# A hybrid encoder layer: token-major attention product, state-group output matrices on VectorE, two-level recurrence

## The chip, the cores and the metric

One core of a Trainium2 chip runs the whole layer as one program. TensorE (PE in the profile) multiplies matrices, its weight loads are listed apart as PEld, VectorE (DVE) and ScalarE (ACT) do elementwise work, GpSimd (POOL) does some more, and SyncE (SP) issues transfers. The metric is the device time of one execution in microseconds (us).

## The reference

One layer with 256 tokens of width 2048 in float32. `w_in` projects to q, k, v and u, each 1024 wide. Three things matter here. The attention group has 16 heads of 64:

```python
scores = einsum(q, k) * 64 ** -0.5 + rel_bias          # band of 64-token chunks, masked
probs = softmax(scores)
out = einsum(probs, v)
```

The state group has 64 channel groups, each driving a 64-dim complex diagonal state, with the pairs (state, group) spread over 128 partitions and 32 columns:

```python
s[l] = a * s[l-1] + B u[l]                             # complex, a per state
y = Re(C s) + d_skip * u ;  y = gelu(y) ; y = y * sigmoid(y @ w_glu + b_glu)
```

Both outputs pass an RMS norm over all 1024 channels, are concatenated, multiplied by `w_out` and added to `alpha * x`; then come a layer norm, a gated FFN of width 5632 with a causal convolution over three tokens, and a second layer norm.

## The kernel before

Weights stream from HBM in chunks of 128 x 1024 float32. Each chunk is split so that two fast products stand for a float32 one: ScalarE casts it to a high part (`hi`, L163), VectorE subtracts to get the low part (`lo`, L164), and TensorE multiplies both (L209 with 512 moving columns and L211 with 256, eight times per chunk, in `mm_a`; L245, L247, L249 in `mm_b`). 104 such chunks make up the first 400 us: v (numbers 0 to 7 and 24 to 31), u (8 to 23), kq (32 to 63: four for each pair of heads, two for k and two for q), then `w_out`'s attention half (64 to 79), the gate of the state group (80 to 87), `w_out`'s state half (88 to 103). The FFN follows, to 1150 us.

`run` (L167) walks over the chunks: it splits chunk j+3, starts the transfer of chunk j+7, issues chunk j's products, and then lets every side job issue one step. Side jobs are generators: parameters of the state group, local states (`s5_loc`, whose products `ll`, L764, are slipped between a chunk's products), stacked kernels, output matrices (`s5_cm`, L909 to L914, on GpSimd), the recurrence (`s5_scan`, L819 to L822) and one attention job for each pair of heads. `paced` deals out a list of small operations, so many us of them per step. Four pairs of hi and lo buffers are in flight. A scheduler then sorts the instructions of each engine by readiness and priority, so that chunks 38 and 39 stand before 36 and 37 on TensorE, and 42 before 40; on the chip each engine works down its own list strictly in order.

The state group cuts the 256 tokens into 64 blocks of 4. `ll` gives each block's own end state; the recurrence then walks over the 64 blocks, 63 steps of four VectorE operations on 128 x 64 elements, each element of `X` 256 bytes from the next. `s5_y` multiplies entering states (`X`) by the output matrices (`CM`) and adds the block's own part.

An attention job for a pair of heads: scores (`S`, L1012, L1013), bias and row maximum on VectorE (L1021, L1022), exponentials on ScalarE (L1024), division by the row sums on VectorE (L1029, L1031), transposes on TensorE (`T`, L1036 to L1038), copy to `pT` (L1040), product with v (`O`, L1048, L1050): weights are v's 64 columns of a head, the moving matrix is `pT` with 256 and then 128 tokens. The result is channel-major, as `w_out`'s product wants it. Its squares are summed on GpSimd (`sqa`, L979), and four TensorE products with a column of ones give the RMS norm (L990). Float32 products on TensorE count as two instructions in the profile.

Of the kernel before, what the change touches and what calls it, by code (L numbers as in the profile page):

```python
# [12 lines left out]
F32 = mybir.dt.float32  # L13
# [3 lines left out]
ALU = mybir.AluOpType  # L17
# [101 lines left out]
class Builder:  # L119
# [172 lines left out]
    def plan_phase1(self):  # L292
# [155 lines left out]
        self.sqa = ap.tile([P, SEQ], F32, name="sqa")  # L448
# [24 lines left out]
    def evac_u(self, f, ps):  # L473
        nc = self.nc
        t = self.evac_ab(ps, f"ub{f}")
        u = self.t1([P, 4, 64], f"ut{f}")
        nc.vector.tensor_tensor(u[:, ::-1].rearrange("p t c -> p c t"), ps[:, 0:SEQ].rearrange("p (c t) -> p c t", t=4),
                                t.rearrange("p (c t) -> p c t", t=4), op=ALU.add)
        with self.tc.high_priority(300):
            self.put_u(f, u)  # L480

# [67 lines left out]
    def s5_params(self):  # L549
# [152 lines left out]
        cA = self.cA = ap.tile([P, 2, NP_], F32, name="cA")  # L702
        cB = self.cB = ap.tile([P, 2, NP_], F32, name="cB")
        ops.append((0.2, lambda: V.tensor_copy(cA[:, 0], PA[:, 0, 3])))
        ops.append((0.2, lambda: V.tensor_copy(cA[:, 1], PA[:, 0, 3])))
        ts(cB[:, 0], PA[:, 1, 3], -1.0, MUL)
        ops.append((0.2, lambda: V.tensor_copy(cB[:, 1], PA[:, 1, 3])))

        ts(self.sc[:, 1], self.sc[:, 1], -1.0, MUL)
        yield from self.paced(ops, 1.7)  # L710
# [27 lines left out]
    def s5_loc(self):  # L738
# [20 lines left out]
        def ll(q, ri):  # L759
            def mm(i, g2):  # L760
                if i == 0 and g2 == 0:
                    st[1] = self.bank((3, 4)[ri], f"ll{q}{ri}")
                r = slice(64 * g2, 64 * g2 + 64)
                nc.tensor.matmul(st[1][r, 64 * i:64 * i + 64], lhsT=loc[:, q % 2, ri, i, r], rhs=self.up[:, q * 8 + i],  # L764
                                 start=True, stop=True, tile_position=(0, 64 * g2))

            def evac():
                nc.scalar.copy(self.X[:, ri, q * 8:q * 8 + 8], st[1].rearrange("p (i c) -> p i c", c=64))
            for i in range(8):
                for g2 in range(2):  # L770
                    put(lambda i=i, g2=g2: mm(i, g2), 0.25)
            put(evac, 0)
# [15 lines left out]
        while self.mb_ready < 4 or self.up_ready < 1:  # L788
            yield
        self.X = bp.tile([P, 2, NP_, 64], F32, tag="d2", name="X")  # L790
        yield from drained()
        yield
        both(ll, 0)
# [13 lines left out]
        yield  # L807

    def s5_scan(self):
        while not self.loc_done:  # L810
            yield
        V, X, ap = self.nc.vector, self.X, self.ap_

        def step(c):
            s = X[:, :, :, c]
            t = X[:, :, :, c + 1]
            u = ap.tile([P, 2, NP_], F32, tag="su", bufs=2, name=f"su{c}")
            w = ap.tile([P, 2, NP_], F32, tag="sw", bufs=2, name=f"sw{c}")
            V.tensor_tensor(u, s[:, ::-1], self.cB, op=ALU.mult)  # L819
            V.tensor_tensor(w, s, self.cA, op=ALU.mult)  # L820
            V.tensor_tensor(u, u, t, op=ALU.add)
            V.tensor_tensor(t, w, u, op=ALU.add)  # L822
# [53 lines left out]

    def s5_cm(self):
        nc, bp, ap = self.nc, self.bp, self.ap_
        Gp = nc.gpsimd
        self.CM = []  # L880
        while not self.par_done:
            yield
# [3 lines left out]
        for pg in range(4):  # L886
# [19 lines left out]
            ci = self.sc[:, 1, pr].unsqueeze(2).broadcast_to(sh)  # L906
            for ri in range(2):

                Gp.tensor_tensor(t0, cr if ri == 0 else ci, ar, op=ALU.mult)  # L909
                Gp.tensor_tensor(t1, ci if ri == 0 else cr, ai, op=ALU.mult)  # L910
                for g2 in range(2):
                    r = slice(64 * g2, 64 * g2 + 64)
                    o = self.CM[pg][r, ri].rearrange("p c (e g q) -> p g c e q", g=2, q=SG)[:, g2]
                    Gp.tensor_tensor(o, t0[r], t1[r], op=ALU.add if ri == 0 else ALU.subtract)  # L914
                yield
            self.cm_ready = pg + 1

    def s5_y(self):
        nc, bp = self.nc, self.bp
        X, Kt, CM, up = self.X, self.Kt, self.CM, self.up  # L920
        for pg in range(4):
            while self.cm_ready <= pg:
                yield
            if pg == 0:
                ysh = self.ysh = bp.tile([P, 8, SEQ], F32, tag="d4b", name="ysh")
            ps = self.bank((3, 4)[pg % 2], f"y{pg}")
            for f in range(2):
                for i in range(4):
                    m = slice(32 * i, 32 * i + 32)
                    for t in range(3):  # L930
                        for r in range(4):
                            l = 4 * f + r
                            pr = 8 * pg + l
                            o = ps[32 * r:32 * r + 32, f * SEQ + i * 64:f * SEQ + (i + 1) * 64]
                            if t == 0:
                                a = dict(lhsT=Kt[:, pr // 16, m, pr % 16], rhs=up[:, pr])
                            else:
                                a = dict(lhsT=CM[pg][:, t - 1, l, m], rhs=X[:, t - 1, pr, 0:63])
                                o = o[:, 1:64]
                            nc.tensor.matmul(o, start=t == 0, stop=t == 2, tile_position=(0, 32 * r), **a)  # L940
                nc.vector.tensor_copy(ysh[:, 2 * pg + f].rearrange("p (c i) -> p i c", i=4),
                                      ps[:, f * SEQ:(f + 1) * SEQ].rearrange("p (i c) -> p i c", i=4))
# [41 lines left out]

    def rms(self, w):
        nc = self.nc
        acc = (self.sqa, self.sqs)[w]
        ps = self.bank((7, 7)[w], f"rms{w}")
        for tt in range(2):
            nc.tensor.matmul(ps[:, tt:tt + 1], lhsT=acc[:, tt * P:(tt + 1) * P], rhs=self.ones, start=True, stop=True)  # L990
        r = self.rs[:, 2 * w:2 * w + 2]
        half = (1.0, 0.5)[w]
        nc.scalar.activation(r, ps[:, 0:2], AF.Sqrt, bias=self.eps, scale=half * half / AW)
        nc.vector.reciprocal(r, r)
        if w == 1:
            nc.vector.tensor_scalar(r, r, half, None, op0=ALU.mult)
        yield


    def attention(self, j):  # L1000
# [12 lines left out]
            nc.tensor.matmul(ps[:, 256:384], lhsT=qt[:, 0:P], rhs=kz[h][:, 0:P], start=True, stop=True)  # L1013

        def soft(h):
            ps, b = st["S", h], st["b", h]
            s = ap.tile([P, 384], F32, tag="sT", bufs=2, name=f"sT{j}{h}")
            m = ap.tile([P, 8], F32, tag="mx", bufs=2, name=f"mx{j}{h}")
            spans = ((0, 256), (256, 384))
            for t, (a, e) in enumerate(spans):  # L1020
                nc.vector.tensor_tensor_reduce(s[:, a:e], ps[:, a:e], b[:, 256 - (e - a):], 1.0, -3e38, ALU.add, ALU.max, m[:, t:t + 1])  # L1021
            nc.vector.tensor_scalar(m[:, 2:4], m[:, 0:2], -1.0, None, op0=ALU.mult)  # L1022
            for t, (a, e) in enumerate(spans):
                nc.scalar.activation(s[:, a:e], s[:, a:e], AF.Exp, bias=m[:, 2 + t:3 + t], accum_out=m[:, 4 + t:5 + t])  # L1024
            st["s", h], st["m", h] = s, m

        def norm(h):
            s, m = st["s", h], st["m", h]
            nc.vector.reciprocal(m[:, 6:8], m[:, 4:6])  # L1029
            for t, (a, e) in enumerate(((0, 256), (256, 384))):  # L1030
                nc.vector.tensor_scalar(s[:, a:e], s[:, a:e], m[:, 6 + t:7 + t], None, op0=ALU.mult)  # L1031

        def trans(h):
            s = st["s", h]
# [32 lines left out]
        yield  # L1067
        soft(0)
        yield
        norm(0)  # L1070
        soft(1)
        yield
        trans(0)
        norm(1)
        yield
        pv(0)
        trans(1)
        if j < 7:
            yield
        pv(1)  # L1080
        yield
        while self.cm_ready < 4:
            yield
# [255 lines left out]
```

## Time and profile before

| | us |
|---|---|
| median of 3 runs | 1151.32 (1151.24 to 1151.71) |
| profiled execution, its own time | 1152.07 |
| its span in the trace | 1150.3 |
| busy in the span: TensorE | 1115.6 (97%) |
| VectorE | 775.0 (67%) |
| ScalarE | 563.4 (49%) |
| GpSimd | 123.3 (11%) |

The shares are means over stages with different limits. The page also gives 40 slices of 28.8 us, each digit a tenth; the lowest busy digit of TensorE behind the first slice, 5, is that of slice 6 (143.8 to 172.5 us).

### The profile page before, as it was taken

Reading aid. Unit: us, or ns where it says so; the run is one execution under the profiler, and the core shown is the slowest. Engines: PE = TensorE matmul, PEld = TensorE weight load, DVE = VectorE, ACT = ScalarE, POOL = GpSimd, SP = SyncE. Lnnn points to the kernel's source line nnn. Section 1 sums busy time; section 2 is a strip of 40 time slices with the busy share of each in tenths; the row PEclk is TensorE's granted clock in tenths of the full one; section 3 lists DMA queues with packets and bytes.
Section 4 is the critical chain, followed back from the end, with each engine's and each line's share of the span. In section 5 each row is a group of like instructions: output and inputs, shape, how many; then the busy total and the mean of one; then the engine's idle time right before and its main releaser. Section 6 shows DMA issues by size and latency. Waiting matters only on the chain.

```text
span 1150.3 us, 17982 instructions
## 1 busy us (share of the span) xinstructions
PE 1115.6 (97%) x6936; PEld 944.2 (82%) x6936; DVE 775.0 (67%) x1379; ACT 563.4 (49%) x849; POOL 123.3 (11%) x113
## 2 busy tenths in 40 slices
PE   8999959999999999999999999999999999999996
PEld 6887748887787888888888888888888888888885
DVE  7993399995678876666666666666666475454555
ACT  5454325553667465555555555555555343343450
POOL 2031870000002000000000000000000550000002
PEclk9999979999999999999999999999999999999998
DMA  8886324553566456666666666666656876666661
GB/s 301 277 236 156 102 87 130 156 155 104 215 192 192 162 163 185 184 185 187 190 187 186 186 185 187 191 185 184 184 185 188 319 211 195 198 188 198 187 198 74
DMA packets 61573, 212.04 MB, mean 184 GB/s; under 512 B 7344, under 2 KB 10800, under 8 KB 60592
## 3 DMA queue, kind: packets, MB, share of 16 engines
q1 hardware_dynamic: 59728, 204.18, 58.0%
q0 software_dynamic: 1472, 6.29, 1.7%
q8 instruction: 54, 0.88, 0.4%
q10 hardware_dynamic: 288, 0.43, 0.1%
q14 instruction: 31, 0.25, 0.1%
HBM read 207.46 MB, written 3.41 MB: 183 GB/s over the span
## 4 chain that ended last, share of the span: by engine, by line
PE 91%; DVE 6%; ACT 1%; issue 1%; DMA 1%; SPq 0%; POOL 0%; ACTq 0%; POOLq 0%
PE f L231 28%; PE f L224 15%; PE d L247 7%; PE d L249 7%; PE d L245 7%; PE kq L209 4%; PE u L209 2%; PE kq L211 2%; DVE lo L164 2%; PE oa L245 1%; PE oa L247 1%; PE u L211 1%; PE oa L249 1%; PE glu L209 1%; PE os L249 1%; PE v L247 1%
## 5 line engine op out<-in xcount | busy, mean ns | idle before, releaser
L164 DVE TENSOR_TENSOR lo<-raw,hi 128x1024 fp32r<-128x1024 f32 (+1 forms) x358 | 448.0, 1254 | 230.0 <-ACT hi L163 226.0
L163 ACT CAST hi<-raw 128x1024 fp32r<-128x1024 f32 (+1 forms) x358 | 374.6, 1047 | 290.2 <-PE d L249 110.5
L231 PE MATMUL f<-x1s,hi 128*128 128x512 f32 (+1 forms) x1408 | 487.2, 396 | 1.5 <-DVE x1s L1161 1.5
L224 PE MATMUL f<-x1s,lo 128*128 128x256 f32 x1408 | 380.0, 281 | 0.0
L231 PEld LDWEIGHTS f<-x1s,hi 128*128 128x128 f32 x1408 | 258.7, 188 | 57.6 <-DVE x1s L1161 1.8
L224 PEld LDWEIGHTS f<-x1s,lo 128*128 128x128 f32 x1408 | 265.8, 189 | 8.6
L247 PE MATMUL d<-lo,hid 128*128 128x512 f32 (+1 forms) x360 | 133.4, 371 | 0.0
L245 PE MATMUL d<-hi,hid 128*128 128x512 f32 (+1 forms) x360 | 133.4, 370 | 0.0
L249 PE MATMUL d<-hi,hid 128*128 128x512 f32 (+1 forms) x360 | 133.3, 370 | 0.0
L209 PE MATMUL kq<-xs,hi 128*128 128x512 f32 x240 | 90.1, 413 | 3.1 <-DVE qt L505 3.1
L245 PEld LDWEIGHTS d<-hi,hid 128*128 128x128 f32 x360 | 67.8, 188 | 11.8
L247 PEld LDWEIGHTS d<-lo,hid 128*128 128x128 f32 x360 | 67.8, 188 | 11.7
L249 PEld LDWEIGHTS d<-hi,hid 128*128 128x128 f32 x360 | 67.8, 188 | 11.5
L211 PE MATMUL kq<-xs,lo 128*128 128x256 f32 x240 | 69.3, 289 | 0.0
L1255 POOL DMA_DIRECT2D gb<-rows x4 | 2.2, 562 | 531.6 <-PE f L231 531.6
L209 PEld LDWEIGHTS kq<-xs,hi 128*128 128x128 f32 x240 | 45.8, 191 | 14.5 <-DVE qt L505 3.5
L1269 ACT COPY ga<-f 128x256 f32<-128x256 f32 x44 | 16.5, 374 | 83.3 <-PE f L231 83.3
L1276 DVE TENSOR_TENSOR gp<-f,ga 128x256 f32<-128x256 f32 x44 | 18.7, 426 | 45.6 <-ACT ga L1269 45.6
L1269 ACT COPY va<-f 128x256 f32<-128x256 f32 x44 | 16.4, 373 | 66.2 <-PE f L231 66.2
L1288 DVE TENSOR_TENSOR va<-f,va 128x256 f32<-128x256 f32 x44 | 18.7, 425 | 43.3 <-ACT va L1269 43.3
L211 PEld LDWEIGHTS kq<-xs,lo 128*128 128x128 f32 x240 | 46.0, 192 | 0.9
L209 PE MATMUL u<-xs,hi 128*128 128x512 f32 x120 | 43.5, 401 | 0.0
(215 smaller groups left out, 1416.6 us busy)
## 6 DMA issues: line engine op xcount, KB each, us to landing
raw<-wf SPq DMA_DIRECT2D x176, 512.0 KB, 3.7
raw<-wd SPq DMA_DIRECT2D x88, 512.0 KB, 4.2
raw<-wkq SPq DMA_DIRECT2D x32, 512.0 KB, 3.7
raw<-wo SPq DMA_DIRECT2D x32, 512.0 KB, 4.2
raw<-wu SPq DMA_DIRECT2D x16, 512.0 KB, 5.0
raw<-wv SPq DMA_DIRECT2D x15, 512.0 KB, 6.1
raw<-wg SPq DMA_DIRECT2D x8, 512.0 KB, 4.2
gb<-rows POOLq DMA_DIRECT2D x4, 1024.0 KB, 12.6
```

The source lines that it names most:

```text
L163: self.nc.scalar.copy(hi[:, c], raw[:, c])
L164: self.nc.vector.tensor_tensor(lo[:, c], raw[:, c], hi[:, c].bitcast(F32), op=ALU.subtract)
L209: nc.tensor.matmul(ps, start=first and kk == 0, stop=False, **h)
L211: nc.tensor.matmul(ps[:, 0:SEQ], start=False, stop=False, **l)
L224: nc.tensor.matmul(th(ps), lhsT=lo[:, w], rhs=th(x), start=False, stop=False)
L231: nc.tensor.matmul(ps[:, c], lhsT=hi[:, w], rhs=x[:, c], start=start and part is None, stop=stop)
L245: nc.tensor.matmul(ps, lhsT=ah, rhs=wh, start=first and kk == 0, stop=False)
L247: nc.tensor.matmul(ps, lhsT=ah, rhs=wl, start=False, stop=False)
L249: nc.tensor.matmul(ps, lhsT=al, rhs=wh, start=False, stop=last and kk == 1)
L1269: self.nc.scalar.copy(tv, v[:, :, 1])
L1276: nc.vector.tensor_tensor(g[:, 2:].rearrange("p (t c) -> p t c", t=2), p0, t, op=ALU.add)
L1288: nc.vector.tensor_tensor(tv, p0, tv, op=ALU.add)
```

## The change

Three parts. First, the product with v takes `pT` as weights (three blocks of 128 tokens) and moves v's 64 columns of a head, so that `O` comes out token-major; the division by the row sums is one multiplication of the pair's `O` (128 x 256) instead of four of the probabilities; ScalarE's squares sum along the row into `ssq`; and two more transposes per pair make the output channel-major. The RMS norm of the attention half becomes one reduction. Second, the arithmetic of the output matrices moves from GpSimd to VectorE; GpSimd keeps their memsets. Third, the 64 blocks become 8 runs of 8 neighbouring ones, and the columns are stored run-minor: `X` holds the states in the order (k, b), with b the run. Seven large multiply-adds of 128 x 512 run all 8 runs side by side, seven small ones (128 x 64) join the runs, and seven large ones add what enters each run, by a table of powers (`QR`, `QI`). `ll`'s evacuation writes to shifted places, with the last of each run to `L8`, and u and y are permuted to fit.

```diff
 def rms(self, w):
-        ps = self.bank((7, 7)[w], f"rms{w}")
-        for tt in range(2):
-            nc.tensor.matmul(ps[:, tt:tt + 1], lhsT=acc[:, tt * P:(tt + 1) * P], rhs=self.ones, ...)
+        if w == 0:
+            nc.vector.tensor_reduce(r, self.ssq, axis=mybir.AxisListType.X, op=ALU.add)
...
 def s5_params
-        ts(cB[:, 0], PA[:, 1, 3], -1.0, MUL)
+        for n in (1, 2, 4):
+            tt(s0, ar, br, MUL)
+            tt(s1, ai, bi, MUL)
+            tt(QR[:, 0, :, n:2 * n], s0, s1, SUB)
+            tt(s0, ar, bi, MUL)
+            tt(s1, ai, br, MUL)
+            tt(QI[:, 1, :, n:2 * n], s0, s1, ADD)
...
 def s5_loc (ll's evacuation)
-                nc.scalar.copy(self.X[:, ri, q * 8:q * 8 + 8], st[1].rearrange("p (i c) -> p i c", c=64))
+                v = st[1].rearrange("p (i c) -> p i c", c=64)
+                nc.scalar.copy(self.X[:, ri, q * 8:q * 8 + 8, 8:64], v[:, :, 0:56])
+                nc.scalar.copy(self.L8[:, ri, q * 8:q * 8 + 8], v[:, :, 56:64])
...
 def s5_scan
-        yield from self.paced([(1.0, lambda c=c: step(c)) for c in range(63)], 2.5)
-        for _ in range(2):
-            yield
+        def madd(cost, o, s, ar, ai, shape, add=None):
+                V.tensor_tensor(u, s[:, ::-1], ai, op=ALU.mult)
+                V.tensor_tensor(w, s, ar, op=ALU.mult)
+                V.tensor_tensor(u, u, add, op=ALU.add)
+                V.tensor_tensor(o, w, u, op=ALU.add)
+        for k in range(2, 9):
+            madd(2.7, row(k), row(k - 1), bc(QR, 0), bc(QI, 0), sh)
+        for b in range(7):
+            madd(1.1, X[:, :, :, 0, b + 1], X[:, :, :, 0, b], one(QR, 7), one(QI, 7), [P, 2, NP_], L8[:, :, :, b])
+        for k in range(1, 8):
+            madd(2.7, row(k), row(0), bc(QR, k - 1), bc(QI, k - 1), sh)
+        yield from self.paced(ops, 1.6)
...
 def s5_cm
-                Gp.tensor_tensor(t0, cr if ri == 0 else ci, ar, op=ALU.mult)
+                V.tensor_tensor(t0, cr if ri == 0 else ci, ar, op=ALU.mult)
-                    Gp.tensor_tensor(o, t0[r], t1[r], op=ALU.add if ri == 0 else ALU.subtract)
+                    V.tensor_tensor(o, t0[r], t1[r], op=ALU.add if ri == 0 else ALU.subtract)
...
 def attention
-            nc.vector.reciprocal(m[:, 6:8], m[:, 4:6])
-            for t, (a, e) in enumerate(((0, 256), (256, 384))):
-                nc.vector.tensor_scalar(s[:, a:e], s[:, a:e], m[:, 6 + t:7 + t], None, op0=ALU.mult)
...
-            nc.tensor.matmul(o[:, 0:256], lhsT=v[:, 0, c0:c0 + 64], rhs=pt[:, 0:256], ...)
-            nc.tensor.matmul(o[:, 128:256], lhsT=v[:, 1, c0:c0 + 64], rhs=pt[:, 256:384], ...)
+            nc.tensor.matmul(o[0], lhsT=pt[:, 0:128], rhs=v[:, 0, c], start=True, stop=True)
+            nc.tensor.matmul(o[1], lhsT=pt[:, 128:256], rhs=v[:, 0, c], start=True, stop=False)
+            nc.tensor.matmul(o[1], lhsT=pt[:, 256:384], rhs=v[:, 1, c], start=False, stop=True)
+        def norm():
+            nc.vector.reciprocal(m[:, 0:4], m[:, 8:12])
+            nc.vector.tensor_tensor(a.rearrange("p (g c) -> p g c", c=64), ..., op=ALU.mult)
+            for t in range(2):
+                nc.scalar.activation(q[:, r], a[:, r], AF.Square, accum_out=self.ssq[:, t, j:j + 1])
...
 (evac)
+            for t in range(2):
+                nc.tensor.transpose(ps[:, P * t:P * t + P], st["a"][:, P * t:P * t + P], self.ident)
-            self.square(self.sqa, ps, j)
```

The new lines move instructions on every engine, since the scheduler sorts them anew. Three places follow, as the programs have them. On TensorE, the last 64 of the local products `ll` stand before between the products of chunks 38 and 39, mostly one at a time (xs are the tokens, up the blocks' inputs):

```order
L209 MATMUL kq_1595<-xs,hi_1474 128x512
L764 MATMUL ll_1375<-up,loc 64x64
L211 MATMUL kq_1595<-xs,lo_1475 128x256
L764 MATMUL ll_1375<-up,loc 64x64
L209 MATMUL kq_1595<-xs,hi_1474 128x512
```

Now they stand between the products of chunk 34 alone (the evacuation of chunk 33 just ahead of them), four or five at a time:

```order
L206 MATMUL kq_1292<-xs,lo_1197 128x256
L207 MATMUL kq_1292<-xs,hi_1196 128x512
L209 MATMUL kq_1352<-xs,hi_1261 128x512
L778 MATMUL ll_1354<-up,loc 64x64 x5
L211 MATMUL kq_1352<-xs,lo_1262 128x256
L778 MATMUL ll_1354<-up,loc 64x64 x4
```

All 64 now stand in chunk 34, between sixteen products of the chunk. On VectorE, between the splits of chunks 42 and 43 (`lo`), before: the first two heads' divisions (L1031, on `sT`) and two steps of the recurrence.

```order
L164 TENSOR_TENSOR lo_1635<-raw_1429,hi_1634 128x1024
L1029 RECIPROCAL mx_1583<-mx_1583 128x2
L1022 TENSOR_SCALAR mx_1628<-mx_1628 128x2
L820 TENSOR_TENSOR sw_1513<-X,cA 128x64
L1031 TENSOR_SCALAR sT_1582<-sT_1582,mx_1583 128x256
L1031 TENSOR_SCALAR sT_1582<-sT_1582,mx_1583 128x128
L821 TENSOR_TENSOR su_1512<-su_1512,X 128x64
L822 TENSOR_TENSOR X<-sw_1513,su_1512 128x64
L819 TENSOR_TENSOR su_1518<-X,cB 128x64
L1029 RECIPROCAL mx_1628<-mx_1628 128x2
```

The same place now, from the split of chunk 42 to the evacuation of pair 1's k (`kz`): the divisions are gone, the last piece of the output matrices (L943, L944, L948) and large multiply-adds (L844 to L847, scratch in `kcm`) have come.

```order
L164 TENSOR_TENSOR lo_1613<-raw_1455,hi_1612 128x1024
L1062 TENSOR_SCALAR mx_1573<-mx_1573 128x2
L847 TENSOR_TENSOR X<-kcm 128x64x8
L943 TENSOR_TENSOR kcm<-prm 128x512
L944 TENSOR_TENSOR kcm<-prm 128x512
L1090 RECIPROCAL mx_1573<-mx_1573 128x4
L948 TENSOR_TENSOR CM_1517<-kcm 64x32x16 x2
L164 TENSOR_TENSOR lo_1642<-raw_1490,hi_1641 128x1024
L844 TENSOR_TENSOR kcm<-X,QI 128x512
L845 TENSOR_TENSOR kcm<-X,kcm 128x512
L846 TENSOR_TENSOR kcm<-kcm,X 128x512
L506 SCALAR_TENSOR_TENSOR qt<-kq_1585,qb_1634 128x256
```

The piece L943 to L948 is the eighth and last of its kind; the seven others stand ahead of the split of chunk 41. On TensorE again, the first head's transposes and product, before, with all of chunk 37 ahead of them:

```order
L207 MATMUL kq_1480<-xs,hi_1324 128x512
L1036 MATMUL T_1677<-ident,sT_1582 128x128
L1037 MATMUL T_1677<-ident,sT_1582 128x128
L1038 MATMUL T_1677<-ident,sT_1582 128x128
L1048 MATMUL O_1721<-pT_1681,vtok 64x256
L1050 MATMUL O_1721<-pT_1681,vtok 64x128
```

Now a quarter of chunk 37 stands between the two, and the product has three parts:

```order
L1073 MATMUL T_1668<-ident,sT_1572 128x128
L209 MATMUL kq_1492<-xs,hi_1346 128x512
L211 MATMUL kq_1492<-xs,lo_1347 128x256
L206 MATMUL kq_1492<-xs,lo_1347 128x256
L207 MATMUL kq_1492<-xs,hi_1346 128x512
L1084 MATMUL O_1714<-vtok,pT_1672 128x64
L1085 MATMUL O_1714<-vtok,pT_1672 128x64
L1086 MATMUL O_1714<-vtok,pT_1672 128x64
```

What follows on TensorE, up to chunk 44: before, the second head, three products of chunk 42, chunks 40 and 41, the rest of 42, and 43, with pair 1's scores between; now, the second head, chunks 42, 43, 40 and 41, pair 1's scores and both of its heads' transposes, and the two transposes of pair 0's output.

## Rows read from the trace of the kernel before

**Rows 1.** The page: granted clock in 40 slices, and the chain by engine.
```profile
PEclk9999979999999999999999999999999999999998
PE 91%; DVE 6%; ACT 1%; issue 1%; DMA 1%; SPq 0%; POOL 0%; ACTq 0%; POOLq 0%
```

**Rows 2.** Windows: stretch, its length, busy time of each engine, PEclk, DMA.
```profile
core 0: us, PE busy (x) PEld busy (x) DVE busy (x) ACT busy (x) POOL busy (x), PEclk, DMA share, GB/s
124.67:142.52 17.85, 17.85 (x162) 11.84 (x161) 2.87 (x3) 4.98 (x7) 14.95 (x13) 1.00 0.32 95
146.67:149.57 2.90, 2.90 (x19) 2.42 (x17) 2.87 (x7) 0.00 (x0) 2.76 (x3) 1.00 0.45 117
146.67:181.84 35.17, 23.09 (x121) 18.06 (x120) 34.27 (x90) 9.67 (x24) 19.31 (x15) 0.76 0.27 76
149.70:171.40 21.70, 9.62 (x44) 6.48 (x44) 21.36 (x41) 4.82 (x14) 16.42 (x13) 0.61 0.26 75
172.00:262.00 90.00, 88.86 (x582) 73.32 (x581) 88.83 (x356) 49.52 (x112) 3.75 (x5) 1.00 0.49 147
```

**Rows 3.** Waits, 140 to 185 us: total, times, longest.
```profile
PE T L1036 <- DVE sT L1031: 9.2, 3, 6.3
```

**Rows 4.** VectorE's timeline: start, length, line, tile; POOL busy at 162, not at 142.
```profile
142.62 1.23 DVE L164 TENSOR_TENSOR lo<-raw,hi 128x1024 fp32r<-128x1024 f32 x1 [8.46 <-ACT hi L163]
143.76 0.26 DVE L819 TENSOR_TENSOR su<-X,cB 128x64 f32<-128x64 f32 x1
143.94 0.26 DVE L820 TENSOR_TENSOR sw<-X,cA 128x64 f32<-128x64 f32 x1
144.73 0.27 DVE L819 TENSOR_TENSOR su<-X,cB 128x64 f32<-128x64 f32 x1
...
162.16 2.14 DVE L164 TENSOR_TENSOR lo<-raw,hi 128x1024 fp32r<-128x1024 f32 x1
```

**Rows 5.** VectorE's timeline, large products of the setup.
```profile
58.59 0.70 DVE L682 TENSOR_TENSOR mbt<-prm 128x512 f32<-128x512 f32 x1
59.19 0.70 DVE L682 TENSOR_TENSOR MB<-prm 128x512 f32<-128x512 f32 x1
```

**Rows 6.** Groups by line, VectorE: count | busy, mean ns | idle before.
```profile
L563 DVE TENSOR_TENSOR prm<-prm 128x32 f32<-128x32 f32 x65 | 9.0, 190 | 0.1
L1021 DVE CUSTOM_DVE_ANT_0 sT<-S,bd 128x256 f32<-128x256 f32 (+1 forms) x32 | 11.1, 353 | 0.3 <-PE S L1013 0.3
```

**Rows 7.** TensorE's timeline: products ll between products of a chunk, grouped, then single.
```profile
98.34 0.51 PE L247 MATMUL v<-lo,xs 128*128 128x512 f32 x1
98.78 0.45 PE L764 MATMUL ll<-up,loc 128*64 128x64 f32 x8
99.16 0.50 PE L249 MATMUL v<-hi,xs 128*128 128x512 f32 x1
...
137.56 0.50 PE L209 MATMUL kq<-xs,hi 128*128 128x512 f32 x1
137.99 0.33 PE L764 MATMUL ll<-up,loc 128*64 128x64 f32 x2
```

**Rows 8.** TensorE's timeline: the first transpose inside chunk 44, and its wait.
```profile
183.74 0.33 PE L1036 MATMUL T<-ident,sT 128*128 128x128 f32 x1 [0.81 <-DVE sT L1031]
```

**Rows 9.** TensorE's timeline: a head's product; four loads of 128 columns; sixteen transposes.
```profile
207.47 0.65 PE L1048 MATMUL O<-pT,vtok 128*64 128x256 f32 x2
207.95 0.38 PE L1050 MATMUL O<-pT,vtok 128*64 128x128 f32 x2
208.27 0.50 PE L209 MATMUL kq<-xs,hi 128*128 128x512 f32 x1
...
364.99 0.61 PE L990 MATMUL rms<-ones,sqs 128*128 128x1 f32 x4 [1.21 <-POOL sqs L979]
365.46 0.49 PE L249 MATMUL os<-hi,gathl 128*128 128x512 f32 x1
...
388.17 2.02 PE L1153 MATMUL lt<-ident,res 128*128 128x128 f32 x16
```

More of the change, by code (lines that the diff above doesn't have):

```diff
@@ L476, in evac_u @@
         u = self.t1([P, 4, 64], f"ut{f}")
-        nc.vector.tensor_tensor(u[:, ::-1].rearrange("p t c -> p c t"), ps[:, 0:SEQ].rearrange("p (c t) -> p c t", t=4),
-                                t.rearrange("p (c t) -> p c t", t=4), op=ALU.add)
+        v = u[:, ::-1].rearrange("p t (k b) -> p b k t", b=8)
+        nc.vector.tensor_tensor(v, ps[:, 0:SEQ].rearrange("p (b k t) -> p b k t", k=8, t=4),
+                                t.rearrange("p (b k t) -> p b k t", k=8, t=4), op=ALU.add)
         with self.tc.high_priority(300):
@@ L790, in s5_loc @@
         self.X = bp.tile([P, 2, NP_, 64], F32, tag="d2", name="X")
+        nc.gpsimd.memset(self.X[:, :, :, 0], 0.0)
         yield from drained()
@@ L811, in s5_scan, with f @@
             yield
[L812 to L822, printed above, removed]
-        yield from self.paced([(1.0, lambda c=c: step(c)) for c in range(63)], 2.5)
-        for _ in range(2):
-            yield
+        V = self.nc.vector
+        X = self.X.rearrange("p r c (k b) -> p r c k b", b=8)
+        L8, QR, QI = self.L8, self.QR, self.QI
+        ops = []
+        def madd(cost, o, s, ar, ai, shape, add=None):
+            n = math.prod(shape[1:])
+            add = o if add is None else add
+            def f():
+                u, w = (self.kcm[:, c:c + n].rearrange("p (r x) -> p r x", r=2) for c in (1024, 1536))
+                if len(shape) == 4:
+                    u, w = (t.rearrange("p r (c b) -> p r c b", b=shape[3]) for t in (u, w))
+                V.tensor_tensor(u, s[:, ::-1], ai, op=ALU.mult)
+                V.tensor_tensor(w, s, ar, op=ALU.mult)
+                V.tensor_tensor(u, u, add, op=ALU.add)
+                V.tensor_tensor(o, w, u, op=ALU.add)
+            ops.append((cost, f))
+        sh = [P, 2, NP_, 8]
+        one = lambda q, k: q[:, :, :, k]
+        bc = lambda q, k: one(q, k).unsqueeze(3).broadcast_to(sh)
+        row = lambda k: L8 if k == 8 else X[:, :, :, k]
+        for k in range(2, 9):
[5 more added lines that the diff above has]
+        yield from self.paced(ops, 1.6)
         yield from self.s5_y()
@@ L878, in s5_cm @@
         nc, bp, ap = self.nc, self.bp, self.ap_
-        Gp = nc.gpsimd
+        Gp, V = nc.gpsimd, nc.vector
         self.CM = []
@@ L986, in rms @@
         nc = self.nc
-        acc = (self.sqa, self.sqs)[w]
-        ps = self.bank((7, 7)[w], f"rms{w}")
-        for tt in range(2):
-            nc.tensor.matmul(ps[:, tt:tt + 1], lhsT=acc[:, tt * P:(tt + 1) * P], rhs=self.ones, start=True, stop=True)
         r = self.rs[:, 2 * w:2 * w + 2]
         half = (1.0, 0.5)[w]
-        nc.scalar.activation(r, ps[:, 0:2], AF.Sqrt, bias=self.eps, scale=half * half / AW)
+        if w == 0:
+            nc.vector.tensor_reduce(r, self.ssq, axis=mybir.AxisListType.X, op=ALU.add)
+            src = r
+        else:
+            src = self.bank(7, f"rms{w}")[:, 0:2]
+            for tt in range(2):
+                nc.tensor.matmul(src[:, tt:tt + 1], lhsT=self.sqs[:, tt * P:(tt + 1) * P], rhs=self.ones, start=True, stop=True)
+        nc.scalar.activation(r, src, AF.Sqrt, bias=self.eps, scale=half * half / AW)
         nc.vector.reciprocal(r, r)
@@ L1017, in soft @@
             s = ap.tile([P, 384], F32, tag="sT", bufs=2, name=f"sT{j}{h}")
[L1018 to L1028, printed above, removed]
-            nc.vector.reciprocal(m[:, 6:8], m[:, 4:6])
-            for t, (a, e) in enumerate(((0, 256), (256, 384))):
-                nc.vector.tensor_scalar(s[:, a:e], s[:, a:e], m[:, 6 + t:7 + t], None, op0=ALU.mult)
+            if h == 0:
+                st["m"] = ap.tile([P, 12], F32, tag="mx", bufs=2, name=f"mx{j}")
+            m = st["m"]
+            spans = ((1, 0, 256), (0, 256, 384))
+            for t, a, e in spans:
+                c = 2 * h + t
+                nc.vector.tensor_tensor_reduce(s[:, a:e], ps[:, a:e], b[:, 256 - (e - a):], 1.0, -3e38, ALU.add, ALU.max, m[:, c:c + 1])
+            nc.vector.tensor_scalar(m[:, 4 + 2 * h:6 + 2 * h], m[:, 2 * h:2 * h + 2], -1.0, None, op0=ALU.mult)
+            for t, a, e in spans:
+                c = 2 * t + h
+                nc.scalar.activation(s[:, a:e], s[:, a:e], AF.Exp, bias=m[:, 4 + 2 * h + t:5 + 2 * h + t], accum_out=m[:, 8 + c:9 + c])
+            st["s", h] = s
         def trans(h):
@@ L1069, in attention @@
         yield
-        norm(0)
         soft(1)
         yield
+        if j < 7:
+            yield
         trans(0)
-        norm(1)
         yield
@@ L1080, in attention @@
         pv(1)
+        norm()
         yield
```

44 lines of the change are left out of this document (26 added, 18 removed).

## The prediction

> **What bounds the kernel now.** I read the page first. In the chain of waits TensorE holds 91% of the span and VectorE 6%, and the granted clock has one hole, slices 5 and 6 (143.8 to 172.5 us) [rows 1]. So only what lets TensorE run earlier, or gives it less, counts, and VectorE's busy share says little. Windows come next. From 149.70 to 171.40 TensorE is busy for 9.62 of 21.70 us, VectorE for 21.36, GpSimd for 16.42, and the mean clock is 0.61 [rows 2]. The waits name the cause on TensorE's side: it waited 9.2 us in three waits, once 6.3, for VectorE's divided probabilities `sT` (L1031) [rows 3]. VectorE's timeline shows why it is late: a split (`lo`) takes 1.23 us at 142.62 and 2.14 at 162.16, where GpSimd is computing the output matrices [rows 4]. VectorE's work there is not much, it is slow. Behind the hole, from 172 to 262 us, TensorE is busy for 88.86 of 90 us and VectorE for 88.83 [rows 2]: VectorE is full but TensorE doesn't wait. Ahead of it, from 124.67 to 142.52, TensorE is full and VectorE busy for only 2.87 of 17.85 us.
>
> The sum is made in the profiled execution (1152.07 us, 0.75 above the median of 1151.32). I follow TensorE to one point, the start of chunk 44, and then count what differs behind it.
>
> **Local products.** Before, chunks 38 and 39 with the 64 `ll` take 17.85 us [rows 2]; the products stand mostly singly, 0.43 us for a chunk's product and then an `ll` [rows 7]. The new order puts four `ll` between neighbours. Such a group exists in the trace: 0.44 us for a 512-column product and 0.38 for four `ll` (eight instructions) [rows 7]. With 0.32 for a 256-column product (an estimate between 0.28 and 0.44), chunk 34 takes 8 x (0.44 + 0.38 + 0.32 + 0.38) = 12.2 us, and another chunk without `ll` takes 2.90 as chunk 37 does [rows 2]: 15.1 against 17.85, a gain of 2.8. Chunk 37 began 4.15 us behind the end of that stretch, at 146.67, and I put its start at 143.8 now.
>
> **The hole.** From 143.8 on VectorE's own list decides, as the order rows show: large multiply-adds stand between the splits and softmax steps that TensorE needs. Up to the division of pair 0's output, on which TensorE's transposes just ahead of chunk 44 wait, it holds:
>
> - five splits (42 to 46): 1.14 us apart (142.62 to 143.76) [rows 4], 5.7;
> - 25 operations on 128 x 512, 21 of the recurrence and four of the last output matrix: 0.60 apart [rows 5], 15.0;
> - delays where an operation reads its forerunner's result: a step of the recurrence takes 0.97, while two independent starts are 0.18 apart [rows 4], so 0.97 - 4 x 0.18 = 0.25 for the two dependent ones; six such groups, 1.5;
> - three small steps of 0.97 [rows 4], 2.9;
> - 17 small operations of the attention (eight maxima, four negations, qt, two kz, a reciprocal, the division), none priced above the maxima's mean of 0.353 [rows 6], less 0.10 each by which neighbours overlap (0.70 busy, 0.60 apart [rows 5]): 4.3.
>
> Together 29.4 us, so the division ends at 173.2, and with two transposes (0.13 each [rows 9]) and a handover chunk 44 starts at about 173.6. TensorE's own work in that stretch is five chunks of 2.90, two scores, four heads' transposes and two products: some 20 us, so it still waits for about 10, in pieces under 3 us (for the exponentials, pair 1's kz, and its probabilities). Before, chunk 44 starts at 181.84 (146.67 + 35.17 [rows 2]); the new order has two heads' transposes done by then which the old one has not, worth the 0.81 us wait behind it [rows 8] and 6 x 0.13: 183.4. So TensorE arrives 9.8 us earlier, of which 2.8 come from the local products. GpSimd's 16 us of arithmetic are gone from here; all but the last of eight pieces are done on VectorE ahead of chunk 41's split, where it had been idle for 15 of 17.85 us [rows 2].
>
> What price the large operations have is the greatest unknown, since no row shows X's pattern with 8 elements in a run. From below: the contiguous 0.60. From above: a step's operation has 64 elements, each 256 bytes from the next, and starts 0.18 after its neighbour; a contiguous one of 32 is busy for 0.19 [rows 6], so it starts about 0.09 after, and by 0.60 for 512 the slope is 1.06 ns an element, which makes 0.125 for 64. Stride costs 0.055 for 64 elements, 0.86 ns each; were all 512 to pay it, an operation would take 1.04. I take 0.60, the row with the same count of elements, because seven of eight neighbours are contiguous; if only the first of each run paid it, 25 operations would cost 1.4 us more, which the range holds.
>
> The Trainium skill, in "SBUF — State Buffer", section "Door 1: The DMA port swizzle (why `[64,N]` ≈ `[32,N]`)", says that accesses within one 16-byte line run at full speed and each crossing to a new line pays, unless at least two hit each line. By that rule steps of one element per line pay, as the 0.18 us show, and X's new runs of 8 (two full lines) pay nothing, so the sum would stay as it is; no row shows such a run.
>
> **The product.** Before, a head's `O` takes 0.80 us (207.47 to 208.27): two passes of 256 columns at 0.24 and two of 128 at 0.16 [rows 9]. Now six passes of 64 columns with 128 weight columns each. Extrapolating the two shapes gives 0.12 a pass; four products with 128 weight columns and one moving column stand 0.118 apart (364.99 to 365.46) [rows 9]. The two rows agree: 0.71, and with the entry of the next product (about 0.14, an estimate from 0.61 busy against 0.47) 0.85. Behind chunk 44 there are 14 heads: 14 x 0.05 = +0.7. From below, were only moving columns to count (0.06, a quarter of 0.24), it would be -0.30 a head, -4.2; from above, at the 0.153 that a pass of those four is busy, +0.26, +3.6. I take +0.7.
>
> **Transposes and norm.** Two more transposes per pair at 0.126 (2.02 for sixteen [rows 9]) and their entry, 0.3; seven pairs behind chunk 44: +2.1. They wait for the division, which now stands behind the product; TensorE has a chunk's work in between, and without this cover each pair would cost about 0.6. The four RMS products go: -0.47.
>
> **VectorE behind chunk 44.** It had some 54 steps of 0.97, 52 us, in its full 90 us; now four steps and seven large multiply-adds, 4 + 28 x 0.60 + 7 x 0.25 = 22.6. It loses 30 us of work there, so TensorE stays the bound. The divisions and GpSimd's sums were hidden and I price their loss at nothing; ScalarE's two squares per pair replace one, at 49% busy. The state group's y comes some seven chunks earlier, beside kq chunks; that can save a few tenths of waiting, which I leave out. Setup's 18 more small operations on powers stand where VectorE has gaps: nothing.
>
> **Sum.** -9.8 + 0.7 + 2.1 - 0.5 = -7.5; for handovers on the new waits I give 0.5 back: -7.0. The profiled execution would take 1145.1, the median 1144.4.
>
> **Rivals.**
>
> A. VectorE doesn't bind in the hole. If the large operations are no hindrance, TensorE's 20 us of work from 143.8 are through by about 165, 8 us earlier than I say: 1136. For it: TensorE has several chunks to reorder around a wait. Against: the list is fixed, and 29.4 us of it stand ahead of chunk 44.
>
> B. The clock stays down. TensorE's waits of 2 to 3 us could leave it at 1.2 GHz from about 152 on; in the hole before, a mean of 0.61 was granted with TensorE busy for less than half [rows 2]. Its 14 us of work left there would take twice as long; ten of these fall into waits, so about 4 us are lost: 1148. For it: TensorE is again idle for a third. Against: the longest wait is half of the 6.3 of before.
>
> C. The hole moves rather than shrinks. The pieces of output matrices on VectorE delay the splits of chunks 36 to 41, and TensorE waits for them ahead of 143.8. Seven pieces are 17 us, beside splits and evacuations; if 7 of these can't be hidden, nothing is gained: 1151. Against it: 15 us of idle VectorE in 17.85 [rows 2].
>
> D. Slower: strided large operations. At 1.04 us, 21 of them add 9.2 us in the hole, and the 28 behind it add 12.3, of which about 9 find VectorE free in time: 3 more, so 1144.4 + 12 = 1156. It decides from the point where the price is 0.88: 0.28 x 25 = 7.0 eats the gain. For it: 0.18 against 0.125 for single strided elements. Against it: runs of eight.
>
> **How the numbers follow.** My forecast has a chance of 0.59 (its own range 1140 to 1149), A 0.11, B 0.09, C 0.10, D 0.11. 0.2% is 2.3 us, about what a measurement of this kernel tells from no change. Faster: 0.57 of the forecast, A, B and a little of C: 0.77. Within 0.2%: the rest of the forecast and of C, a little of D: 0.12. Slower: D and the costly ends of the product: 0.11. The range of 8 in 10 goes from A's 1136 to C's 1151.5; it leaves out D.
>
> **What would show it.** In the new trace, GpSimd should have no arithmetic between 120 and 175 us; the 64 `ll` should take some 12 us with chunk 34; large multiply-adds should start 0.60 apart; chunk 44 should start near 173.6, with TensorE idle for 9 to 11 us in the 30 before; a head's product should take 0.85. I am wrong if a large operation takes over 0.8, if TensorE waits for splits ahead of 143 us, or if the clock stays at half past 160.

## The result and the profile after

The changed kernel takes 1140.18 us (median of four, 1139.1 to 1142.15), and the kernel before, run beside it, 1151.51. The ratio is 0.9903 with a 95% interval of 0.9891 to 0.9914, a gain of 11.3 us by the medians. I had forecast 1144.4, a gain of 7.0: the sign was right and the time lies in my range, but the profile shows that two parts of the sum, the hole and what lies behind it, were off in opposite directions.

The page after, granted clock and chain, answers to [rows 1]:

```profile
PEclk9999979999999999999999999999999999999998
PE 93%; DVE 4%; ACT 1%; issue 1%; DMA 1%; SPq 0%; POOL 0%; ACTq 0%; POOLq 0%
```

The row of the clock is the same as before, digit for digit, with one slice (the sixth) at 7: at 28.5 us a slice it doesn't show what changed. VectorE's part of the chain falls from 6% to 4%. Windows of the kernel after (stretch, its length, busy time of PE, PEld, DVE, ACT and POOL, granted clock, DMA) answer to [rows 2]:

```profile
150.00:155.00 5.00, 2.64 (x8) 2.26 (x9) 5.00 (x10) 0.00 (x0) 0.00 (x0) 0.52 0.39 108
155.00:160.00 5.00, 5.00 (x25) 4.38 (x24) 3.86 (x10) 1.05 (x1) 0.00 (x0) 0.80 0.10 26
160.00:165.00 5.00, 1.55 (x9) 0.92 (x7) 4.02 (x7) 2.41 (x6) 0.00 (x0) 0.88 0.48 137
165.00:170.00 5.00, 4.34 (x13) 3.76 (x14) 4.50 (x10) 0.00 (x0) 0.00 (x0) 0.50 0.20 76
143.25:176.49 33.24, 24.85 (x134) 20.34 (x132) 28.74 (x69) 11.62 (x32) 0.00 (x0) 0.79 0.39 116
```

GpSimd is idle, as forecast, and the hole is still there, though smaller: TensorE is busy for 2.64 of 5 us from 150 and 1.55 from 160, and its products run at half clock (1.2 in place of 2.4 GHz) from 152 to 157 and from 165 to 170. The last line is the stretch from chunk 37 to chunk 44. TensorE's waits from 142 to 178 us (total, times, longest) answer to [rows 3]:

```profile
PE kq L209 <- DVE qt L506: 2.6, 1, 2.6
PE kq L209 <- DVE kz L501: 2.5, 2, 2.1
PE T L1071 <- ACT sT L1065: 2.4, 2, 2.0
```

The longest wait falls from 6.3 to 2.6 us, and three of 2.0 to 2.6 are left. I had named those for the exponentials (`sT`) and for pair 1's `kz`; `qt` I had only among VectorE's small operations. VectorE's timeline after shows three neighbours of a large multiply-add, for the price that I called the greatest unknown [rows 5]:

```profile
157.13 0.69 DVE L844 TENSOR_TENSOR kcm<-X,QI 128x512 f32<-128x512 f32 x1
157.74 0.69 DVE L845 TENSOR_TENSOR kcm<-X,kcm 128x512 f32<-128x512 f32 x1
158.34 0.68 DVE L846 TENSOR_TENSOR kcm<-kcm,X 128x512 f32<-128x512 f32 x1
```

They start 0.60 apart and are busy for 0.69, as the contiguous products are, so X's runs of eight cost nothing. With that the trace agrees with what I had cited of the Trainium skill, "SBUF — State Buffer", section "Door 1: The DMA port swizzle (why `[64,N]` ≈ `[32,N]`)". A head's product on TensorE after, with the last product of a chunk ahead and the first one behind, answers to [rows 9]:

```profile
183.25 0.39 PE L207 MATMUL kq<-xs,hi 128*128 128x512 f32 x1
183.48 0.33 PE L1084 MATMUL O<-vtok,pT 128*128 128x64 f32 x2
183.65 0.39 PE L1085 MATMUL O<-vtok,pT 128*128 128x64 f32 x2
183.87 0.39 PE L1086 MATMUL O<-vtok,pT 128*128 128x64 f32 x2
184.07 0.48 PE L209 MATMUL kq<-xs,hi 128*128 128x512 f32 x1
```

From 183.48 to 184.07 are 0.59 us, against 0.80 before and my 0.85. Chunk 44 starts here:

```profile
176.49 0.47 PE L209 MATMUL kq<-xs,hi 128*128 128x512 f32 x1 [0.42 <-DVE kz L501]
```

That is 6.9 us ahead of its counterpart (183.4) and not the 9.8 that I had summed; the gate's first product starts at 314.64 against 325.55, 10.9 ahead. So 6.9 us come from the hole and the local products, and 4.0 from behind it, where I had expected to lose 2.3 (and 0.5 more for handovers on the new waits). From the gate on the two kernels run 10.9 to 11.0 apart to the end.

### The profile page after: what moved, and what is told of

Same layout as the page of the kernel before. It is cut to its first block, busy times and chain, and to the rows that moved or that the text cites. A ratio compares the mean times of both kernels' runs of the same rounds, so it can differ in the third digit from the quotient of the medians.

```text
span 1139.3 us, 17905 instructions
## 1 busy us (share of the span) xinstructions
PE 1110.3 (97%) x6980; PEld 948.8 (83%) x6980; DVE 774.4 (68%) x1230; ACT 566.6 (50%) x882; POOL 75.5 (7%) x75
## 4 chain that ended last, share of the span: by engine, by line
PE 93%; DVE 4%; ACT 1%; issue 1%; DMA 1%; SPq 0%; POOL 0%; ACTq 0%; POOLq 0%
PE f L231 29%; PE f L224 15%; PE d L245 7%; PE d L249 7%; PE d L247 7%; PE kq L209 5%; PE u L209 2%; PE kq L211 2%; PE oa L249 1%; PE oa L245 1%; PE oa L247 1%; PE u L211 1%; PE glu L209 1%; DVE lo L164 1%; PE os L249 1%; PE os L245 1%
## 5 line engine op out<-in xcount | busy, mean ns | idle before, releaser
L209 PE MATMUL kq<-xs,hi 128*128 128x512 f32 x240 | 92.8, 422 | 5.1 <-DVE qt L506 2.6
```

The lines of the kernel that those rows point to most:

```text
L209: nc.tensor.matmul(ps, start=first and kk == 0, stop=False, **h)
```

## The experiments

The change has three parts that can be built apart. The first four kernels ask which of them the time comes from. Each measurement below is the median, with the ratio to the kernel before and its 95% interval. Theory 1 was that GpSimd's arithmetic beside VectorE made the hole, and that each part has its own price; the rival was that the hole is VectorE's load, which the two-level recurrence relieves.

**cm_alone.** The kernel before, with only this changed:

```diff
-                Gp.tensor_tensor(t0, cr if ri == 0 else ci, ar, op=ALU.mult)
+                V.tensor_tensor(t0, cr if ri == 0 else ci, ar, op=ALU.mult)
...
-                    Gp.tensor_tensor(o, t0[r], t1[r], op=ALU.add if ri == 0 else ALU.subtract)
+                    V.tensor_tensor(o, t0[r], t1[r], op=ALU.add if ri == 0 else ALU.subtract)
```

> The kernel before with the arithmetic of the output matrices on VectorE and nothing else. Theory 1 (GpSimd's concurrent arithmetic is what makes VectorE slow in the hole): splits there fall from 2.1 to 1.2 us, divisions from 2.6 to under 1, and about half of the hole goes, 5 to 9 us: about 1144.5. Rival (the hole is VectorE's total load; the matrices' 14 to 19 us come on top of it): 1149 to 1156, no faster.

Measured: 1134.81 (0.9853, 0.9837 to 0.9868), a larger gain than theory 1 gave, and larger than that of the whole change. Two of its windows, and a split:

```profile
150.00:155.00 5.00, 4.60 (x25) 3.78 (x26) 4.77 (x21) 0.73 (x2) 0.00 (x0) 1.00 0.42 111
160.00:165.00 5.00, 4.03 (x24) 3.23 (x22) 4.97 (x23) 5.00 (x15) 0.00 (x0) 1.00 0.46 161
```

```profile
158.12 1.22 DVE L164 TENSOR_TENSOR lo<-raw,hi 128x1024 fp32r<-128x1024 f32 x1
```

TensorE is busy and its clock whole. VectorE is as full as before (4.97 of 5), but its work is through in time: the split takes 1.22 us, not 2.14 [rows 4].

**product_alone.** The kernel before, with the token-major product, `norm` and the two transposes of the change's `attention` and `rms`, and nothing else.

> The kernel before with the token-major product, its norm and the transposes, and nothing else. Theory 1: a head's product costs 0.61 us in place of 0.80 and the transposes 0.16 a pair, so about 2.1 us go on TensorE outside the hole; in the hole the four slowed divisions go too, 3 to 5 us: about 1145. Rival (the price of the prediction, 0.85 a head and 0.3 a pair): +2.3 outside, so 1149 to 1151.

Measured: 1152.83 (1.001, 1.0 to 1.0019): no gain. TensorE's waits from 142 to 178 us:

```profile
PE kq L209 <- DVE qt L504: 7.1, 1, 7.1
PE T L1037 <- ACT sT L1031: 5.0, 1, 5.0
```

The divided probabilities are gone from the waits, and the hole stays: exponentials and `qt` are late in their place, since all of VectorE is. Theory 1 falls on this kernel: the divisions were what TensorE happened to wait for, not the cause. The rival's 1149 to 1151 is nearer, though 1152.83 lies outside it too, and the price behind it is refuted by the product's 0.59 us above.

**product_and_cm.** The changed kernel with the old recurrence and the old order of columns:

```diff
-        yield from self.paced(ops, 1.6)
+        yield from self.paced([(1.0, lambda c=c: step(c)) for c in range(63)], 2.5)
```

> The changed kernel with the old recurrence of 63 small steps and the old order of columns. Theory 1 (the two-level recurrence is worth little in time, since it puts 21 large operations in the hole): 1139 to 1143, within 0.3% of the changed kernel's 1140.2. Rival (the recurrence is what made room on VectorE): 1146 or more.

Measured: 1136.73 (0.9868, 0.9853 to 0.9883). It is faster than the changed kernel (the intervals of the ratios, 0.9853 to 0.9883 and 0.9891 to 0.9914, lie apart), so theory 1 was right in that the recurrence isn't what gains, and too mild: where the change puts it, the two-level form costs about 3.5 us against the old steps. Of its windows and its waits up to 262 us:

```profile
150.00:155.00 5.00, 4.38 (x14) 3.58 (x14) 4.73 (x22) 0.48 (x1) 0.00 (x0) 0.50 0.39 106
155.00:160.00 5.00, 5.00 (x30) 4.41 (x28) 3.22 (x15) 1.05 (x1) 0.00 (x0) 0.94 0.04 8
```

```profile
PE O L1050 <- ACT pT L1041: 5.0, 6, 1.3
```

By the medians it takes 1.9 us more than cm_alone, but the two intervals overlap, so that isn't clear of noise. In the profiled executions its clock falls to half from 150 to 155 us, and TensorE waits 5.0 us for `pT`; cm_alone's waits in that span were shorter (total, times, longest):

```profile
PE T L1036 <- DVE sT L1031: 2.1, 4, 1.2
PE O L1048 <- ACT pT L1040: 1.8, 2, 1.2
```

**cm_and_scan.** The changed kernel with the product, divisions and RMS norm of before (`sqs` shares `sqa`'s buffer, for room).

> The changed kernel with the old channel-major product and divisions of the probabilities (the new output matrices on VectorE and the new recurrence stay). Theory 1: 0.80 against 0.61 us a head over 16 heads costs 3.0, the transposes saved give 1.3 back, the RMS products cost 0.4, and eight divisions in the hole some tenths: 1142.5 to 1144. Rival (the product changes nothing or harms, by the prediction's price): 1137.5 to 1140.

Measured: 1144.17 (0.9931, 0.9916 to 0.9946), so beside the new recurrence the product gains some 4 us, a little above the expected 2.3 to 3.8. By the medians it changes the time by +1.5, +1.9 or -4.0 us, by what else stands in the list; the first two are at the edge of what these runs tell from nothing. Waits from 142 to 178 us:

```profile
PE kq L209 <- DVE kz L502: 2.1, 2, 1.5
PE O L1082 <- ACT pT L1074: 1.8, 2, 1.2
PE S L1046 <- DVE kz L502: 1.5, 1, 1.5
PE T L1070 <- DVE sT L1065: 1.2, 1, 1.2
```

Theory 2 came from this: what is left of the hole is the recurrence's 21 large operations between the splits of chunks 42 to 46. The next four test both theories.

**cm_gpsimd_busy.** cm_alone, with 32 products on GpSimd that nothing reads:

```diff
+                for _ in range(4):
+                    Gp.tensor_tensor(dum, cr, ar, op=ALU.mult)
                 V.tensor_tensor(t0, cr if ri == 0 else ci, ar, op=ALU.mult)
```

> The kernel with only the output matrices moved to VectorE (cm_alone, 1134.8), where GpSimd in addition computes 32 products of 128 x 512 into a scratch that nothing reads, some 20 us of them from 142 us on. Theory 1 (GpSimd computing beside VectorE slows VectorE): splits of 2 us and a hole return, 1146 to 1153. Rival (the old pieces held up VectorE or TensorE by an order or a wait of their own, not by running beside them): 1134 to 1137.

Measured: 1176.68 (1.0203, 1.0181 to 1.0226). GpSimd's timeline, a split beside it, and a window of each of the two stretches:

```profile
126.41 14.24 POOL L911 TENSOR_TENSOR dum<-prm 128x512 f32<-128x512 f32 x9
166.25 21.07 POOL L911 TENSOR_TENSOR dum<-prm 128x512 f32<-128x512 f32 x16
139.61 2.12 DVE L164 TENSOR_TENSOR lo<-raw,hi 128x1024 fp32r<-128x1024 f32 x1
```

```profile
124.00:142.00 18.00, 7.16 (x61) 4.50 (x59) 17.88 (x14) 1.80 (x3) 15.88 (x12) 0.66 0.24 83
170.00:175.00 5.00, 0.53 (x3) 0.50 (x3) 5.00 (x10) 2.38 (x8) 4.69 (x5) 0.91 0.60 165
```

A hole stands at each of GpSimd's two long stretches: the split is back at 2.12 us, TensorE is busy for 7.16 of 18 us from 124, where it is full in every other kernel, and VectorE for 17.88 with 14 instructions, where cm_alone needs 14.01 for 32. The time is above theory 1's 1146 to 1153; I had foreseen one such stretch, and there are two. That GpSimd's products slow VectorE's work by running beside it is shown, and that this was the hole of the kernel before.

**scan_from_40 and scan_from_44.** The changed kernel, with the recurrence's first step at a later chunk:

```diff
-        self.side(35, self.s5_scan())
+        self.side(44, self.s5_scan())
```

> The changed kernel with the recurrence's side job begun at chunk 40 in place of 35; nothing else. Theory 2 (the large operations of the recurrence are what is left of the hole: they delay TensorE by 2 to 3 us at a time and its clock falls to 1.2 GHz): some of them leave 150 to 170 us, 1135 to 1138. Rival (they cost the same wherever they stand): 1139 to 1142.

> The changed kernel with the recurrence begun at chunk 44, behind the hole. Theory 2: VectorE has slack there, TensorE's waits and the low clock of 150 to 170 us go nearly wholly; cm_alone's 1134.8 less 1 to 3 us for the cheaper product: 1131 to 1135. Rival (large operations hold up a split or a softmax step wherever they stand): 1138 to 1141.

Measured: 1130.32 (0.9809, 0.9794 to 0.9824) from 40, and 1128.75 (0.9803, 0.9787 to 0.982) from 44, both below the expected range. Windows of scan_from_40, then of scan_from_44:

```profile
150.00:160.00 10.00, 9.57 (x47) 8.33 (x48) 7.41 (x18) 2.54 (x7) 0.00 (x0) 0.83 0.27 80
```

```profile
150.00:155.00 5.00, 4.38 (x27) 3.75 (x26) 4.83 (x10) 0.48 (x1) 0.00 (x0) 1.00 0.44 135
165.00:170.00 5.00, 5.00 (x32) 4.47 (x31) 5.00 (x10) 2.77 (x5) 0.00 (x0) 1.00 0.44 137
```

With the recurrence begun at chunk 44 the hole is gone and the clock whole, with VectorE as full as ever (5.00 of 5) but ahead of TensorE; begun at 40, the clock still dips once, to 0.83 over these 10 us. Theory 2 holds: there the same large operations don't hold TensorE up. From 143 us to the gate TensorE's waits fall from 9.6 us (changed kernel) to 2.7 (scan_from_44), and the kq products, which ran partly at half clock, from 77.6 to 72.4. The two starting points, 40 and 44, can't be told apart by their intervals. scan_from_44 beats the changed kernel by 1.0% (1128.75 against 1140.18; the ratios' intervals are 0.9787 to 0.982 and 0.9891 to 0.9914).

**scan_44_old_product.** cm_and_scan, with the recurrence from chunk 44.

> Output matrices on VectorE, the two-level recurrence begun at chunk 44, and the old channel-major product. Theory 2 with the product worth 1 to 3 us on TensorE: 1134 to 1136.5, above scan_from_44. Rival (the product's gain beside the changed recurrence, 4 us between cm_and_scan and the changed kernel, came from the order of the list and not from the product): equal to scan_from_44 within 0.1%, or below it.

Measured: 1136.01 (0.9857, 0.9842 to 0.9872). The product is worth 7 us here, more than the 1 to 3 that I expected. From the starts of TensorE's instructions (each counted up to the next, less its wait) from 143 us to the gate, sixteen heads' products take 12.8 us in the old form and 10.1 in the new, the new transposes 1.3, the attention half of `w_out` 47.6 against 45.7, and waits 5.2 against 2.7. That accounts for 5.8 of some 7. Part of the waits, from scan_44_old_product between 240 and 310 us (scan_from_44 has 0.9 for `ysh` there and none of `issue`):

```profile
PE y L974 <- issue: 2.1, 2, 1.8
PE y L974 <- DVE ysh L975: 1.5, 3, 0.6
```

So the product with its transposes brings 1.4 us (12.8 - 10.1 - 1.3). The rest goes with where the scheduler's list puts y, with the waits, and with the clock behind one of them: after the 1.8 us at 281.18 the mean clock from 280 to 285 us is 0.66, and six of `w_out`'s products take 2.7 us in place of 1.4. What in the product's code moves these was not tried.

**old_scan_from_44.** product_and_cm, with the recurrence from chunk 44: does the two-level form matter?

> Token-major product and output matrices on VectorE as in the changed kernel, but the old recurrence of 63 small steps, begun at chunk 44. Theory 2 (beginning late is what frees the hole; the two-level form is what lets the state group still finish in time: 22 chunks against some 28): the hole goes, but y comes some seven chunks later, close ahead of the gate's chunks: 1130 to 1135, slower than scan_from_44's 1128.75 by 1 us or more. Rival (the form doesn't matter once it begins late): within 0.1% of scan_from_44.

Measured: 1141.14 (0.9905, 0.9888 to 0.9921), 12 us above scan_from_44 and above theory 2's 1130 to 1135. So the form matters once it begins late: y's products now run up to 304 us, beside `w_out`'s, and the gate starts at 314.77 against 302.63. Of these 12 us, waits give 5.4, the kq products 3.4 and `w_out`'s attention half 2.8, counted as above; the clock falls once near 150 us (0.66 from 150 to 155) and once behind a wait of 2.1 us. A window and TensorE's waits from 240 to 315 us:

```profile
240.00:260.00 20.00, 17.55 (x88) 14.40 (x87) 14.70 (x51) 10.15 (x27) 0.00 (x0) 0.91 0.46 125
```

```profile
PE oa L245 <- DVE qt L504: 2.1, 1, 2.1
PE y L939 <- issue: 1.8, 2, 1.3
```

**scan_from_48.**

> The changed kernel with the two-level recurrence begun at chunk 48. Theory 2: nothing is left to free at 150 to 170 us, so no more than 0.15% from scan_from_44's 1128.75 unless y's end then delays the gate. Rival (every large operation that leaves the kq chunks still gives something): 1125 to 1127.

Measured: 1133.2 (0.9837, 0.9823 to 0.9852), slower than from 44 by about 4 us. The rival falls, and so does my 0.15%; only its clause on y's end holds. y's last products start near 290 us in place of 274, and TensorE waits there from 255 to 305 us:

```profile
PE y L973 <- issue: 3.6, 2, 1.8
```

The profile names no releaser for these 3.6 us (`issue`); both stand inside a group of y's products, not ahead of one, and what they are stays open. Behind the second the clock is 0.66 from 285 to 290 us. The recurrence has room on both sides: earlier, it stands in the hole's place; later, y's end does.

## Why the prediction was right, and where not

**What bounds the kernel.** Right, and shown from both sides: without GpSimd's products the hole goes (cm_alone), and with products that nothing reads it returns (cm_gpsimd_busy). One reading was off: the row of the clock has one slice below 9, the sixth, and not two.

**Local products.** Right: in the trace after, groups of four follow each other after 0.81 and 0.70 us in turn (118.91 to 130.26), and chunk 37 starts at 143.3 against my 143.8.

**The hole: the step that failed.** "Together 29.4 us, so the division ends at 173.2" took VectorE's list as work without a wait, and TensorE's own work ("some 20 us") as work at the full clock. The division starts at 175.16 and ends at 175.58. From VectorE's timeline after:

```profile
155.97 0.42 DVE L1061 CUSTOM_DVE_ANT_0 sT<-S,bd 128x256 f32<-128x256 f32 x1 [0.94 <-PE S L1049]
162.12 1.23 DVE L164 TENSOR_TENSOR lo<-raw,hi 128x1024 fp32r<-128x1024 f32 x1 [0.98 <-ACT hi L163]
171.68 0.42 DVE L1061 CUSTOM_DVE_ANT_0 sT<-S,bd 128x256 f32<-128x256 f32 x1 [1.95 <-PE S L1049]
175.16 0.42 DVE L1094 TENSOR_TENSOR at<-O,mx 128x256 f32<-128x256 f32 x1
```

With 0.21 us more, VectorE waited for 4.1 us, mostly for scores that TensorE was late with. From the list's first maximum, at 143.09, to the end of the division are 32.5 us, so the work in it took 28.4: its price, 29.4, was too high by about 1 us and not too low. On TensorE, of the 33.2 us from chunk 37 to chunk 44, 8.4 were waits (I had about 10) and 24.8 work (I had some 20). The work took longer because part of it ran at 1.2 GHz. In TensorE's timeline after, a pair of products takes 0.64 us at 153.17 and 0.35 at 157.37:

```profile
153.17 0.63 PE L209 MATMUL kq<-xs,hi 128*128 128x512 f32 x1
153.60 0.41 PE L211 MATMUL kq<-xs,lo 128*128 128x256 f32 x1
153.81 0.63 PE L209 MATMUL kq<-xs,hi 128*128 128x512 f32 x1
...
157.37 0.39 PE L209 MATMUL kq<-xs,hi 128*128 128x512 f32 x1
157.60 0.28 PE L211 MATMUL kq<-xs,lo 128*128 128x256 f32 x1
157.72 0.39 PE L209 MATMUL kq<-xs,hi 128*128 128x512 f32 x1
```

So the two engines waited for each other in turn: products at half clock followed TensorE's waits, and they made the scores late for which VectorE then waited. Rival B (the clock) happened for two stretches of 4.6 us, and I had put it beside the forecast instead of into it. Chunk 44 also waited for pair 2's two `kz`, which my list left out (they end 0.8 us behind the division).

**Where the recurrence stands.** I counted its 21 operations as part of the hole and never asked what the sum is without them. This is the point that decides the size of the gain: from chunk 35 the two-level form costs 3.5 us against the old steps beside the new product (changed kernel, product_and_cm) and 9.4 beside the old one (cm_and_scan, cm_alone); from chunk 44 it gains 12 (scan_from_44, old_scan_from_44), and 8 against the old steps from chunk 35. Rival A, 1136, is nearly what cm_alone reached; I gave it 0.11 because the list was fixed, which was true of this change alone.

**The product.** The sum had +0.7 for 14 heads; it was -2.6 to -2.9 (0.59 to 0.61 against 0.80). Six passes of 0.098 are 0.59, less than my 0.118 to 0.12 apiece; and I had added 0.14 for the next product's entry to the new form alone, though the old form's 0.80 didn't hold it. There is nothing to add for either: the chunk's first product takes 0.31 us to the next one behind the new product (184.07 to 184.38) as it took 0.33 behind the old.

**Transposes.** +2.1 forecast, 1.1 measured behind chunk 44 (14 at 0.079, entries aside).

**VectorE behind chunk 44.** Right: from 180 to 262 us TensorE is busy for 80.81 of 82 us after, VectorE for 61.30. The earlier y, which I left out, comes with 0.4 us less waiting in y's products (1.2 against 1.6) and 1.3 less on `w_out`'s, but 0.7 more on y's own.

The hole was thus 2.9 us worse than forecast, what lies behind it 6.3 better, and the 0.5 for handovers too much. That the total came within 4.2 us of the forecast is in part luck, since errors of opposite sign cancelled. Rival C (delayed splits ahead of 143 us) didn't happen: TensorE is busy for 18.00 of 18 us from 124. Rival D fell with the 0.60.

## What to carry to other kernels

When an engine is slow, ask first who runs beside it: the same arithmetic moved onto the engine that it disturbs was worth 1.5% by itself, while relieving that engine in other ways (product_alone) was worth nothing. Time each part of a bundled change alone and with each other part; here one part gave more than the whole, and another cost 3.5 us where it was put and gave 8 when begun nine chunks later. In these kernels a faster algorithm for work off the critical path paid only through when it could start and when it had to end, so try its starting point (35, 40, 44, 48 gave 1140, 1130, 1129, 1133) before its form.

## What the runs showed of the hardware

- GpSimd's products of 128 x 512 beside VectorE's: a split of 128 x 1024 took 2.14 us in place of 1.23, and 14 VectorE instructions filled 17.88 of 18 us; a GpSimd memset of 3.5 us beside the small steps of the recurrence (142.72 in the trace before) left them at 0.27 us.
- In the trace before, operations of VectorE that were held up ended with GpSimd's. Two divisions and two of GpSimd's sums:

```profile
153.36 2.64 DVE L1031 TENSOR_SCALAR sT<-sT,mx 128x256 f32<-128x256 f32 x2
153.33 2.59 POOL L914 TENSOR_TENSOR CM<-kcm 64x512 f32<-64x512 f32 x2
```

With GpSimd idle, the first of such a pair took 0.35 us (at 182.62). The maximum (L1021), which reads the scores from PSUM, kept its 0.41 us at 148.70 while GpSimd's sums ran from 147.40 to 150.03. So not every operation was slowed; which are, no run here sorts out.

- A VectorE operation with an operand in runs of eight float32, 256 bytes apart, was busy for 0.69 us on 128 x 512, as a contiguous one is. Single elements 256 bytes apart started 0.18 us apart on 128 x 64, against an estimated 0.125 for neighbours.
- In the changed kernel a wait of 2.6 us, and then two of 2.0 and 2.1 with only three transposes between them, were each followed by 4.6 us of products at the 1.2 GHz level (0.64 a pair). Shorter waits went either way: scan_from_40 and scan_from_44 both have two, 1.8 us together and 1.1 the longest, from 142 to 178 us; in the first the mean clock from 150 to 155 us was 0.66, in the second it stayed at 2.4 GHz. Of the four executions of scan_from_40, two had a mean clock of 0.995 (1130.9 and 1131.2 us) and two of 0.997 (1129.0 and 1129.7).
